# Sixteen loads of 16 to 1 rows that need not end at a row's end, in a log-sum-exp over rows

## Chip, cores, metric

One core of one Trainium2 chip. The metric is device time in microseconds (us), the median of several runs; runs of one kernel here spread over 0.2 to 0.6 us. Times inside a run are counted from the start of its profiled span. A run's reported time is 1.8 us longer than its span.

## The reference

```python
x: (32, 512, 1024) float32, standard normal
max_x = np.max(x, axis=-1, keepdims=True)
out = max_x.squeeze(-1) + np.log(np.sum(np.exp(x - max_x), axis=-1))   # (32, 512) float32
```

That is 16,384 rows of 1,024 elements, 67.1 MB in, 64 KB out. With 128 partitions each holds 128 rows.

## The kernel before

It takes exp without the maximum, sums, takes the logarithm, and guards itself: if a sum is out of range, a slow branch computes everything again. Data come through a ring of 48 row slots per partition. One string is one load. `R6` is six rows exponentiated by one ScalarE instruction and summed by one VectorE reduce; `T2` two rows, exponentiated together, each summed by a VectorE two-input sum of its halves; `A` one row exponentiated and summed by ScalarE alone.

```python
RING = 48
loads = [
    "R6 R5 R5", "R6 R5 R5", "R8 R8", "R8 R4 R4", "R4 R4 R3 R3 A A", "R6 T3 A A A", "R6 A A",
    "R2 A A T2", "R3 R3", "R3", "A A A", "T2 A", "T2", "T2", "T1", "A", "A",
]
...
for i, ops in enumerate(loads):
    size = sum(s for _, s in ops)
    if p + size > RING:
        p = 0
    dma = nc.sync.dma_start(out=ring[:, p : p + size, :], in_=source(c, size)).ins
    for how, s in ops:
        v = ring[:, p : p + s, :]
        sums = sumexp[:, c : c + s]
        if how == "A":
            o = v if c < LAST else last_exp
            exp = nc.scalar.activation(out=o, in_=v, func=AF.Exp, accum_out=sums)
        else:
            exp = nc.scalar.activation(out=v, in_=v, func=AF.Exp)
        ...                          # the reduce or the two-input sums on VectorE
        c += s; p += s
    if c == LATE:                    # 118 rows: first logarithm, first guard check
        ...
```

After the loop:

```python
nc.scalar.activation(out=res[:, W:NC], in_=sumexp[:, W:NC], func=AF.Ln)
nc.sync.dma_start(out=out_rows, in_=res[:, 0:W])
last_store = nc.sync.dma_start(out=out_rest, in_=res[:, W:NC]).ins   # 8 KB: the last store
check(LATE, LAST, 1)                                                 # VectorE, after the last sum
... # small reduce and comparison on VectorE, matmuls, a flag `fine`
all_fine = nc.values_load(fine[0:1, 0:1], engines=ENGINES, ...)      # ScalarE and VectorE read it
with tc.If(all_fine < 1, preferred_fallthrough_block=False):
    ...                                                              # the slow branch
```

## Time and profile before

| | before |
|---|---|
| time, median of 3 | 163.81 us (163.78 to 163.9) |
| span of the profiled run | 161.76 us |
| DMA, first packet to last packet | 1.005 to 157.450 us |
| last load seen landed | 157.954 us |
| last exponential starts | 157.976 us |

The views that show what bounds it are in the prediction. One view of before is shown now: what SyncE waited for at the end (its next step comes at 161.00 in before, 0.76 us ahead of the end of the span; the receiver, what it waited for, us in total, times, longest), and the DMA issue of the last store (KB, us from issue to landing).

```profile
SPq L275 <- DVEq L208: 0.5, 1, 0.5
SPq L275 <- DMA out_dram<-res: 0.4, 1, 0.4
out_dram<-res SPq DMA_DIRECT2D x1, 8.0 KB, 1.6
```

The last thing that SyncE waits for is the 8 KB store, after it has waited for VectorE's branch: in before it has seen everything else by 160.55, and the store at 161.00.

### The profile page before, as it was taken

The numbers are of one execution on the slowest core, as the hardware profiler recorded it, in microseconds if no ns is written. First come the engines' busy times: TensorE is split into PE (matmuls) and PEld (weight loads), VectorE is DVE, ScalarE is ACT, GpSimd is POOL, SyncE is SP. The second block draws the span as 40 slices with busy tenths as digits, with TensorE's granted clock in tenths as the row PEclk, the third lists the DMA queues.
The fourth block names the chain that finished last, engine by engine and source line by source line (L and its number), as shares of the span: only waits on it lengthen the run. The fifth ranks groups of instructions, "written<-read, shape, count | busy, mean of one in ns | idle before, by whom it ended". The sixth has DMA issues, their size and how long they took to land.

```text
span 161.8 us, 221 instructions
## 1 busy us (share of the span) xinstructions
PE 0.8 (0%) x8; PEld 0.3 (0%) x8; DVE 118.5 (73%) x56; ACT 117.2 (72%) x60; POOL 0.2 (0%) x4
## 2 busy tenths in 40 slices
PE   0000000000000000000000000000000000000001
PEld 0000000000000000000000000000000000000000
DVE  0000002999959997299995999999999589799772
ACT  3000069980899609994299924999999999999994
POOL 0000000000000000000000000000000000000000
DMA  7996996997997997998898899889999999999990
GB/s 259 519 519 276 502 519 292 486 519 324 454 519 324 454 519 340 438 519 389 389 519 389 389 519 389 389 389 502 405 389 434 474 389 432 416 428 415 418 368 6
DMA packets 2738, 67.19 MB, mean 415 GB/s; under 512 B 560, under 2 KB 560, under 8 KB 944
## 3 DMA queue, kind: packets, MB, share of 16 engines
q1 hardware_dynamic: 2736, 67.18, 97.0%
q14 instruction: 2, 0.02, 0.0%
HBM read 67.11 MB, written 0.07 MB: 415 GB/s over the span
## 4 chain that ended last, share of the span: by engine, by line
DMA 53%; DVE 35%; ACT 10%; issue 1%; PE 0%
DMA ring<-in_x_dram 53%; DVE sumexp L132 35%; ACT ring L122 9%; ACT ring L120 1%; ACT last_exp L120 0%; PE count L202 0%; DVE fine L203 0%
## 5 line engine op out<-in xcount | busy, mean ns | idle before, releaser
L132 DVE TENSOR_REDUCE sumexp<-ring 128x3 f32<-128x3072 f32 (+5 forms) x21 | 109.5, 5276 | 37.2 <-ACT ring L122 37.2
L122 ACT ACTIVATE ring<-ring 128x3072 f32<-128x3072 f32 (+6 forms) x27 | 100.3, 3763 | 41.4 <-DMA ring<-in_x_dram 41.3
L120 ACT ACTIVATE ring<-ring 128x1024 f32<-128x1024 f32 x14 | 14.6, 1040 | 0.0
L137 DVE SCALAR_TENSOR_TENSOR ring<-ring 128x512 f32<-128x512 f32 x12 | 7.7, 687 | 2.1 <-ACT ring L122 2.1
L120 ACT ACTIVATION_READ_ACCUMULATOR ring<-ring 128x1 f32 x14 | 2.6, 187 | 0.0
L75 ACT ACT_TABLE_LOAD x1 | 1.3, 1283 | 0.8 <-PEq L264 0.8
L102 PE MATMUL count<-far,bad 128*1 128x1 f32 x4 | 0.4, 164 | 158.3 <-DVE clamped L98 158.3
L120 ACT ACTIVATE last_exp<-ring 128x1024 f32<-128x1024 f32 x1 | 1.0, 1027 | 0.0
L137 DVE DVE_READ_ACCUMULATOR ring<-ring 128x1 f32 x12 | 1.0, 83 | 0.0
L76 DVE MEMSET ones<- 128x1 f32 x1 | 0.1, 59 | 0.9 <-PEq L264 0.9
L203 DVE TENSOR_SCALAR fine<-count 1x1 int32<-1x1 f32 x1 | 0.1, 145 | 0.6 <-PE count L202 0.6
L94 DVE TENSOR_SCALAR clamped<-sumexp 128x118 f32<-128x118 f32 (+1 forms) x2 | 0.4, 197 | 0.2
L102 PEld LDWEIGHTS count<-far,bad 128*1 128x1 f32 x4 | 0.2, 81 | 158.4 <-DVE clamped L98 158.4
L98 DVE SCALAR_TENSOR_TENSOR clamped<-clamped,sumexp 128x118 f32<-128x118 f32 (+1 forms) x2 | 0.5, 225 | 0.1
L155 ACT ACTIVATE res<-sumexp 128x112 f32<-128x112 f32 x1 | 0.3, 280 | 0.0
L190 ACT ACTIVATE res<-sumexp 128x16 f32<-128x16 f32 x1 | 0.2, 216 | 0.0
L197 DVE TENSOR_REDUCE bad<-ring 128x1 f32<-128x64 f32 x1 | 0.2, 220 | 0.0
L201 PE MATMUL count<-far,bad 128*1 128x1 f32 x2 | 0.2, 164 | 0.2 <-DVE bad L198 0.2
L202 PE MATMUL count<-ones,sumexp 128*1 128x1 f32 x2 | 0.2, 164 | 0.1
L120 ACT ACTIVATION_READ_ACCUMULATOR last_exp<-ring 128x1 f32 x1 | 0.2, 187 | 0.0
L198 DVE TENSOR_SCALAR bad<-bad 128x1 f32<-128x1 f32 x1 | 0.2, 154 | 0.0
L98 DVE DVE_READ_ACCUMULATOR clamped<-clamped,sumexp 128x1 f32 x2 | 0.2, 82 | 0.0
(7 smaller groups left out, 0.6 us busy)
## 6 DMA issues: line engine op xcount, KB each, us to landing
ring<-in_x_dram SPq DMA_DIRECT2D x1, 6144.0 KB, 28.8
ring<-in_x_dram SPq DMA_DIRECT2D x2, 3072.0 KB, 27.9
ring<-in_x_dram SPq DMA_DIRECT2D x3, 1536.0 KB, 29.2
ring<-in_x_dram SPq DMA_DIRECT2D x1, 4096.0 KB, 27.8
ring<-in_x_dram SPq DMA_DIRECT2D x2, 1024.0 KB, 30.0
ring<-in_x_dram SPq DMA_DIRECT2D x3, 512.0 KB, 25.9
ring<-in_x_dram SPq DMA_DIRECT2D x5, 35.3
out_dram<-res SPq DMA_DIRECT2D x1, 56.0 KB, 8.7
```

The costliest lines, as they stand in the source:

```text
L75: nc.scalar.preload_act_table_set("natural_log_exp_and_others")
L94: nc.vector.tensor_scalar(out=clamped[:, c0:c1], in0=sumexp[:, c0:c1], scalar1=LOW, scalar2=HIGH, op0=ALU.max, op1=ALU.min,)
L98: counted = nc.vector.scalar_tensor_tensor(out=clamped[:, c0:c1], in0=clamped[:, c0:c1], scalar=0.0, in1=sumexp[:, c0:c1], op0=ALU.bypass, ...
L102: nc.tensor.matmul(count, lhsT=bad[:, i : i + 1], rhs=far, start=i == 0, stop=False)
L120: exp = nc.scalar.activation(out=o, in_=v, func=AF.Exp, accum_out=sums)
L122: exp = nc.scalar.activation(out=v, in_=v, func=AF.Exp)
L132: added = [nc.vector.reduce_sum(out=sums, in_=v, axis=AX.X)]
L137: nc.vector.scalar_tensor_tensor(out=lo, in0=lo, scalar=1.0, in1=ring[:, p + r, H:d], op0=ALU.mult, op1=ALU.add, accum_out=sums[:, r : r + 1],
L155: ln = nc.scalar.activation(out=res[:, 0:W], in_=sumexp[:, 0:W], func=AF.Ln)
L190: nc.scalar.activation(out=res[:, W:NC], in_=sumexp[:, W:NC], func=AF.Ln)
L197: nc.vector.reduce_max(out=bad[:, 3:4], in_=last_row[:, 0, 0 : d // 16], axis=AX.X)
L198: nc.vector.tensor_scalar(out=bad[:, 2:3], in0=bad[:, 3:4], scalar1=LOG_LOW, scalar2=None, op0=ALU.is_lt)
```

## The change

Loads are counted in elements, so one may end inside a row. The exponentials take all that has landed, into the unfinished row; the row is summed after the load that completes it. The intent is that ScalarE has as little as possible left when the last loads land, with one load fewer.

```diff
     loads = [
-        "R6 R5 R5", "R6 R5 R5", "R8 R8", "R8 R4 R4", "R4 R4 R3 R3 A A", "R6 T3 A A A", "R6 A A",
-        "R2 A A T2", "R3 R3", "R3", "A A A", "T2 A", "T2", "T2", "T1", "A", "A",
+        (16, "R8 R7 A"), (16, "R8 R7 T1"), (16, "R6 R5 R5"), (16, "R6 R5 R5"), (13.5, "R5 R4 R4"),
+        (12.5, "R7 R6"), (9, "A A A A A A A A A"), (7.5, "R3 R2 R2"), (5.5, "R4 T2"),
+        (4, "A A A A"), (3.5, "T3"), (2.75, "T3"), (2.25, "T2"), (1.5, "T2"), (1, "A"), (1, "A"),
     ]
-    LATE = 118
+    LATE = 119
 ...
-        dma = nc.sync.dma_start(out=ring[:, p : p + size, :], in_=source(c, size)).ins
+        dma = nc.sync.dma_start(out=ring[:, here : here + size], in_=source(done, size)).ins
 ...
             else:
+                upto = end if k + 1 == len(ops) else p + s * d
+                v = ring[:, here:upto]
                 exp = nc.scalar.activation(out=v, in_=v, func=AF.Exp)
+                here = upto
 ...   (the rest turns row indices into element indices)
```

More of the change, by code (lines that the diff above doesn't have):

```diff
@@ L39 @@
     W = NC - B
-    x_rows = x_flat[0 : P * W].rearrange("(p c) d -> p c d", p=P)
-    x_rest = x_flat[P * W : n].rearrange("(p c) d -> p c d", p=P)
+    x_rows = x_flat[0 : P * W].rearrange("(p c) d -> p (c d)", p=P)
+    x_rest = x_flat[P * W : n].rearrange("(p c) d -> p (c d)", p=P)
     out_flat = out.rearrange("a b -> (a b)")
@@ L50 @@
     loads = [
-        "R6 R5 R5", "R6 R5 R5", "R8 R8", "R8 R4 R4", "R4 R4 R3 R3 A A", "R6 T3 A A A", "R6 A A",
-        "R2 A A T2", "R3 R3", "R3", "A A A", "T2 A", "T2", "T2", "T1", "A", "A",
-    ]
-    loads = [[(op[0], int(op[1:] or 1)) for op in load.split()] for load in loads]
-    assert sum(s for ops in loads for _, s in ops) == NC
[3 rows of a table added]
+    ]
+    loads = [
+        (int(size * d), [(op[0], int(op[1:] or 1)) for op in ops.split()]) for size, ops in loads
+    ]
+    assert sum(size for size, _ in loads) == NC * d
+    assert sum(s for _, ops in loads for _, s in ops) == NC
     ENGINES = [mybir.EngineType.Activation, mybir.EngineType.DVE]
-    LATE = 118
+    LATE = 119
     LAST = NC - 1
@@ L62 @@
     psum = ctx.enter_context(tc.tile_pool(name="psum", bufs=1, space=bass.MemoryType.PSUM))
-    ring = big.tile([P, RING, d], fp32, name="ring")
+    ring = big.tile([P, RING * d], fp32, name="ring")
     sumexp = stats.tile([P, NC], fp32, name="sumexp")
@@ L71 @@
     ones = stats.tile([P, 1], fp32, name="ones")
-    last_exp = psum.tile([P, 1, d], fp32, name="last_exp")
+    last_exp = psum.tile([P, d], fp32, name="last_exp")
     count = psum.tile([1, 1], fp32, name="count")
@@ L77, with source @@
     nc.vector.memset(far, 100 * HIGH)
-    def source(c0, size):
-        assert c0 >= W or c0 + size <= W
-        return x_rest[:, c0 - W : c0 - W + size, :] if c0 >= W else x_rows[:, c0 : c0 + size, :]
+    def source(e0, size):
+        assert e0 >= W * d or e0 + size <= W * d
+        return x_rest[:, e0 - W * d : e0 - W * d + size] if e0 >= W * d else x_rows[:, e0 : e0 + size]
     def without_wait(ins, group, reason):
@@ L107 @@
     p = 0
-    for i, ops in enumerate(loads):
-        size = sum(s for _, s in ops)
-        if p + size > RING:
-            p = 0
-        dma = nc.sync.dma_start(out=ring[:, p : p + size, :], in_=source(c, size)).ins
+    here = 0
+    done = 0
+    for i, (size, ops) in enumerate(loads):
+        if here + size > RING * d:
+            assert here == p
+            p = here = 0
+        dma = nc.sync.dma_start(out=ring[:, here : here + size], in_=source(done, size)).ins
         if i == 0:
             first_load = dma
-        for how, s in ops:
-            v = ring[:, p : p + s, :]
+        end = here + size
+        done += size
+        for k, (how, s) in enumerate(ops):
+            rows = ring[:, p : p + s * d].rearrange("p (c d) -> p c d", d=d)
             sums = sumexp[:, c : c + s]
             if how == "A":
+                assert here == p
+                v = ring[:, p : p + d]
                 o = v if c < LAST else last_exp
                 exp = nc.scalar.activation(out=o, in_=v, func=AF.Exp, accum_out=sums)
+                here += d
             else:
+                upto = end if k + 1 == len(ops) else p + s * d
+                v = ring[:, here:upto]
                 exp = nc.scalar.activation(out=v, in_=v, func=AF.Exp)
+                here = upto
+            assert p + s * d <= here <= end
             without_wait(exp, "loads", "the slot's earlier users came before this load")
@@ L131 @@
             if how == "R":
-                added = [nc.vector.reduce_sum(out=sums, in_=v, axis=AX.X)]
+                added = [nc.vector.reduce_sum(out=sums, in_=rows, axis=AX.X)]
             elif how == "T":
                 for r in range(s):
-                    lo = ring[:, p + r, 0:H]
+                    lo = rows[:, r, 0:H]
                     added.append(
                         nc.vector.scalar_tensor_tensor(
-                            out=lo, in0=lo, scalar=1.0, in1=ring[:, p + r, H:d],
+                            out=lo, in0=lo, scalar=1.0, in1=rows[:, r, H:d],
                             op0=ALU.mult, op1=ALU.add, accum_out=sums[:, r : r + 1],
@@ L150 @@
             c += s
-            p += s
+            p += s * d
             last_row = v
+        assert here == end
         tc.add_to_no_dep_group("loads", dma)
@@ L196 @@
     check(LATE, LAST, 1)
-    nc.vector.reduce_max(out=bad[:, 3:4], in_=last_row[:, 0, 0 : d // 16], axis=AX.X)
+    nc.vector.reduce_max(out=bad[:, 3:4], in_=last_row[:, 0 : d // 16], axis=AX.X)
     nc.vector.tensor_scalar(
@@ L214 @@
                     s = min(RING, NC - c0)
-                    v = ring[:, 0:s, :]
+                    v = ring[:, 0 : s * d].rearrange("p (c d) -> p c d", d=d)
                     neg = clamped[:, c0 : c0 + s]
@@ L223 @@
                         nc.scalar.dma_start(
-                            out=ring[:, c1 - c0 : c2 - c0, :], in_=source(c1, c2 - c1)
+                            out=ring[:, (c1 - c0) * d : (c2 - c0) * d],
+                            in_=source(c1 * d, (c2 - c1) * d),
                         ).then_inc(landed, 16)
```

## The prediction

The sum in it came to -0.09 us, from 163.81 to 163.72. Statements that no trace of this case shows are cut out of it, with the cuts marked; no term of the sum is among them, since each was worked out from the trace of before. The figures of that trace, for reading it:

- 1,040 and 7,025 ns are the mean durations of an exponential of one row and of eight. The 0.10 + 0.853 us per row is my estimate; plain exponentials of 2, 3, 4, 5, 6 and 8 rows that follow each other start 1.80, 2.65, 3.51, 4.36, 5.23 and 6.94 us after one another there. Those of one row with its sum start 1.039 us apart (111.549 and 112.588), not 1.036. Reduces of 3, 4, 5, 6 and 8 rows start 3.26, 4.33, 5.39, 6.47 and 8.60 us apart, about 1% more than the 1.055 per row + 0.05 of the walk.
- The first load is issued at 0.00 and its first packet starts at 1.005: the 1 us of issue. The third and the fourth load raise their sixteenth increments at 60.480 and 79.842, 19.36 us apart, as loads of 16 rows do that move one after the other.
- SyncE waited up to 22.7 us for ring slots, and the DMA share was still 1.00 from the first packet to the last.

> **What bounds the kernel now**
>
> I read the page first, then the chain of waits, then the busy time by windows, then the timeline of the last microseconds. The page alone misleads: its chain gives VectorE 35% of the span.
>
> ```profile
> DMA 53%; DVE 35%; ACT 10%; issue 1%; PE 0%
> q1 hardware_dynamic: 2736, 67.18, 97.0%
> ```
>
> The second line is the one that matters: 67.18 MB on one queue keep all 16 DMA engines busy for 97% of the span. To see whether there is a hole anywhere, I cut the span where the first packet starts moving (1.00 us) and where the last packet ends (157.45 us), both read from the trace's records of single packets. Columns: stretch, its length, busy time of PE, PEld, DVE, ACT, POOL, then granted clock, DMA share, GB/s.
>
> ```profile
> 1.00:157.45 156.45, 0.19 (x2) 0.09 (x2) 117.04 (x47) 115.06 (x56) 0.00 (x0) 1.00 1.00 429
> 157.45:161.76 4.31, 0.57 (x6) 0.26 (x6) 1.34 (x8) 1.89 (x5) 0.00 (x0) 1.00 0.04 8
> ```
>
> DMA share 1.00: the loads never pause. So the time is 1.0 us before the first packet, 156.45 us of packets without a hole, and a tail of 4.3 us. DVE's 35% in the chain is only the inferred path by which ring slots came free; it cost nothing, as this piece of the chain in order of time shows (start, length, what):
>
> ```profile
> 27.17 17.35 DVE sumexp L132 x3
> 44.52 0.02 issue
> 44.53 35.31 DMA ring<-in_x_dram
> ```
>
> The fourth load is issued at 44.53 when reduces free its slots, but takes 35.31 us to land, because it queues behind the third load, which is still moving until 60.1. It was ready some 15 us too early; no stall.
>
> What remains is whether the tail begins when the last load lands, or whether ScalarE is then late:
>
> ```profile
> 152.20 4.78 ACT L122 ACTIVATE ring<-ring 128x2048 f32<-128x2048 f32 x3
> 156.88 1.04 ACT L120 ACTIVATE ring<-ring 128x1024 f32<-128x1024 f32 x1
> 157.83 0.19 ACT L120 ACTIVATION_READ_ACCUMULATOR ring<-ring 128x1 f32 x1
> 157.98 1.03 ACT L120 ACTIVATE last_exp<-ring 128x1024 f32<-128x1024 f32 x1
> ```
>
> ScalarE seems busy right up to the last exponential at 157.98. But back-to-back exponentials of one row start 1.036 us apart in this trace, so from 156.88 it could have started at 157.91 or 157.92. The sixteenth semaphore increment of the last load is recorded at 157.954. Hence the landing sets 157.98, by 0.06 us over ScalarE. Taking ScalarE's backlog away alone therefore gains nothing, and the tail after 157.98 (1.15 us of exponential and accumulator, a 0.22 us logarithm, the small store issued at 159.40 and seen landed at 160.99, final barriers) is not touched by the change.
>
> [...]
>
> [...] a packet of 65,536 bytes takes 2.418 us on one engine, 27.1 GB/s, times 16 is 434 GB/s.
>
> [...] Medians here: 4,096 bytes 0.161 us, 8,192 0.312, 12,288 0.461, 24,576 0.913, 49,152 1.815, 65,536 2.418. That is a line, 0.0095 us + 0.1506 us per row of 4 KB, so about 10 ns a packet[...].
>
> [...] Here last packet end to last increment is 157.45 to 157.954, 0.50 us. [...]
>
> [...] 1,040 ns for 1,024 elements[...], 7,025 for 8,192[...]. Issue to issue, I use 0.10 + 0.853 us per row for a plain exponential, and 1.036 for one with its sum.
>
> **The change part by part**
>
> *Seventeen loads become sixteen; bytes are equal (128 rows a partition).* Every load is 128 packets, 8 on each engine, whatever its length; the longest stays 16 rows. From one load's end to the next, the trace has 19.32 us for 16 rows, 9.71 for 8, 7.30 for 6, and about 1.28 for 1 (mean of three): 1.20 us per row plus about 0.09 us per load (8 packets at 10 to 12 ns). One load fewer: -0.09 us. Fractions are multiples of a quarter row, 1,024 bytes, and each stays one run per partition, so 13.5 rows should cost 8 x (0.0095 + 13.5 x 0.1506) = 16.34 us, on the same line.
>
> *Ring reuse.* With 48 slots, the new sizes fill 16+16+16, then 16+13.5+12.5 (six slots unused), then 38 rows. I walked the two engines by row costs (reduce 1.055 us per row + 0.05) and asked when the overlapping reduces free each slot. Load four: free at 45, needed at 60. Load five: 64 against 79. Six: 77 against 96. Seven (9 rows): 97 against 111. Eight: 107.5 against 122. Nine: 112 against 131. Ten: 116 against 137.5; eleven: 124 against 142. The smallest lead is about 14 us. Issue needs 1 us. So the stream should stay without a hole: 0.
>
> *Splitting the exponentials off row ends.* Total ScalarE elements are equal. What changes is that after a short load everything landed is exponentiated at once. I take landings of before at an equal number of loads and shift by 1.20 us a row. Example: before, 123 rows in 13 loads landed at 151.605; now 124.5 rows in 13 loads, so 151.605 + 1.80 = 153.41. Then:
>
> - load 12 (2.75 rows) lands 150.62; ScalarE, free at about 150.6 after the logarithm, works to 150.64 + 0.10 + 2.35 = 153.09;
> - load 13 (2.25) lands 153.41, after ScalarE is idle: starts 153.43, to 155.45;
> - load 14 (1.5) landed 155.30: 155.45 to 156.83;
> - load 15 (1) landed 156.59: 156.83 to 157.87;
> - load 16 (1) lands 156.666 + 1.20 = 157.87: starts at about 157.89.
>
> ScalarE and the last landing meet again within hundredths. The start moves from 157.98 to 157.89: -0.09 us, all from the missing load.
>
> *VectorE's end and the guard.* Load 14's two rows of 0.61 us each come out at 156.94 + 1.31 = 158.25, against 157.99 before. Its check, the small reduction and comparison follow, to about 159.08 instead of 158.82. The last matmul cannot start before ScalarE's sum at about 159.09, so the guard's flag moves by no more than about 0.05 us. SyncE in before had seen everything but the small store by 160.55, and the store at 160.99, so the guard has 0.4 us of slack: 0.
>
> *Instructions.* Reshaped sums (13 one-row two-input sums instead of 12, 19 reduces instead of 21, one-row exponentials with sums 16 instead of 15) shift work between engines with tens of per cent of idle time early on: 0.
>
> Sum: -0.09 us, chosen prediction 163.81 - 0.09 = 163.72 us.
>
> **The rivals**
>
> *Odd packet lengths slow the queue.* Eight of the 16 loads have a fractional length and five end inside a row. For: no such length occurs in before, so nothing measured covers it; 5 ns more in each of the 64 packets an engine gets for them would be +0.3 us (164.0). Against: quarter rows are 1,024 bytes, and lengths from 4 to 64 KB lie on one line.
>
> *A ring wait replaces a row-end wait.* A freshly loaded slot now waits for two exponentials and the reduce over both. For: SyncE's longest wait in before is 22.7 us for reduces, and it issues in order. Against: 14 us of lead everywhere by my walk. If I am wrong by that much, each microsecond of hole adds one: 165 or more.
>
> *ScalarE's backlog was the real bound* and finer loads win 0.3 to 0.5 us: 163.4. For: it has no idle from 138.1 on in before. Against: the 157.954 landing, after which the last exponential starts in 0.02 us.
>
> *ScalarE or VectorE becomes late.* I have ScalarE ready within 0.02 us of the landing; 0.1 us of error in the walk puts the result at 163.8. VectorE would need to be 0.4 us later than I have it.
>
> **Range and chances**
>
> Runs of before spread over 0.12 us, so a step of 0.09 is hardly more than noise. The queue's arithmetic gives a floor of about -0.1 us unless the first load or the skew between engines changes; the rivals reach 0.3 either way. I take 163.45 to 163.92. Two per cent is 3.3 us; only a hole of several microseconds could do that. Faster by over 2%: 0.01; within 2%: 0.98; slower by over 2%: 0.01.
>
> **What would show it right or wrong**
>
> DMA share 1.00 from the first packet to the last, ending at about 157.36; packets of 55,296 bytes at about 2.04 us; ScalarE idle for some 0.3 us before the 2.25-row exponential; the last exponential at 157.9; issue of every load over 10 us before its first packet. Wrong would be a gap between packets, fractional packets above the line, the last exponential well after its landing, or the guard's flag, not the small store, ending the program.

## The result, and the profile after

| | before | after |
|---|---|---|
| time, median of 6 runs each, same rounds | 163.80 us (163.6 to 163.9) | 163.94 us (163.85 to 164.17) |
| ratio | 1 | 1.0012 (1.0000 to 1.0025) |

A ratio is the mean time of one kernel's runs over the mean of the other's runs of the same rounds, so not quite the ratio of the medians. Within 2%, the forecast class; but 163.94 lies just above the range's end of 163.92, and the sign is against the forecast -0.09. The miss of the range is small: a repeat of the same kernel (after_again, below) had a median of 163.82, inside it. The effect is hardly larger than noise, so below I compare single events in the traces rather than times alone.

First the lines of after that answer to those in the prediction: the queues, then the busy time cut at its own first and last packet.

```profile
q1 hardware_dynamic: 2592, 67.18, 96.6%
q14 instruction: 2, 0.02, 0.0%
...
1.02:157.48 156.46, 0.19 (x2) 0.09 (x2) 115.24 (x45) 115.06 (x56) 0.00 (x0) 1.00 1.00 429
157.48:162.14 4.66, 0.43 (x6) 0.22 (x6) 1.68 (x10) 1.82 (x5) 0.00 (x0) 1.00 0.04 7
```

The stream has again no hole (DMA share 1.00, 429 GB/s). It is the tail after it that grew, from 4.31 to 4.66 us. ScalarE at the end of after (start, length, engine, line, instruction, idle time before it):

```profile
153.51 3.50 ACT L137 ACTIVATE ring<-ring 128x2304 f32<-128x2304 f32 x2 [0.24 <-DMA ring<-in_x_dram]
156.92 1.04 ACT L132 ACTIVATE ring<-ring 128x1024 f32<-128x1024 f32 x1
157.86 0.19 ACT L132 ACTIVATION_READ_ACCUMULATOR ring<-ring 128x1 f32 x1
157.96 1.00 ACT L132 ACTIVATE last_exp<-ring 128x1024 f32<-128x1024 f32 x1
```

ScalarE caught up at 153.51, as the change intends, and began the last exponential at 157.96, 0.02 earlier than before. Nothing is lost up to here. VectorE's last row sum is at 157.29 to 157.99 before:

```profile
157.29 0.69 DVE L137 SCALAR_TENSOR_TENSOR ring<-ring 128x512 f32<-128x512 f32 x1
...
157.90 0.08 DVE L137 DVE_READ_ACCUMULATOR ring<-ring 128x1 f32 x1
```

and at 157.66 to 158.36 after:

```profile
157.66 0.68 DVE L154 SCALAR_TENSOR_TENSOR ring<-ring 128x512 f32<-128x512 f32 x1
...
158.27 0.08 DVE L154 DVE_READ_ACCUMULATOR ring<-ring 128x1 f32 x1
```

So VectorE ends 0.37 later. And SyncE's waits and the last store of after:

```profile
SPq L294 <- DMA out_dram<-res: 0.7, 1, 0.7
SPq L294 <- DVEq L226: 0.6, 1, 0.6
out_dram<-res SPq DMA_DIRECT2D x1, 8.0 KB, 2.0
```

The store takes 2.0 us to land instead of 1.6, though it is issued no later (159.36 and 159.40) and nothing in the change touches it. In the traces every load and every store raises its semaphore, the counter that SyncE waits on, 16 times, and has 16 packets of 4 bytes (304 of each for the 19 transfers of before, 288 for the 18 of after). I read this as one increment for each of the 16 DMA engines. The trace's own records of increments and packets, in us from the span's start:

```
                                       before             after
VectorE ends its last row sum          157.987            158.355
8 KB instruction packet, first         159.067-159.635    159.397-159.892
8 KB instruction packet, second        159.595-159.994    159.976-160.443
packets of the last store (64 bytes)   160.239-160.440    160.195-160.500
  15th increment of the store          160.849            160.768
  16th increment of the store          160.985            161.371
end of the span                        161.756            162.143
```

Fifteen increments are there 0.08 us earlier than before; one comes 0.60 us after them. Read by engines, one finishes late. In after the eight data packets of that engine stand alone, one every 7 ns from 160.440, and the second instruction packet ends at 160.443. (The records kept do not number the DMA engines; that the two share one is read from these times.) The packets themselves are little delayed: those of the other fifteen engines, with a 4-byte packet each at the end, are over at 160.409, those of this one at 160.505. But its increment is recorded only 0.87 us after that. That instruction packet is in the page as `q14 instruction`: two packets, 16 KB in all, 0.0% of the DMA time, in both kernels.

**Theory A.** These are fetches of the instruction streams of ScalarE and VectorE. They start when the engines pass a certain place in their streams, near VectorE's last sum, after which both engines go on. VectorE ending 0.37 us later moves its fetch 0.38 us later (159.595 to 159.976), onto the DMA engine and into the moment of the last store, which then completes late.

**Theory B.** The late increment is a chance of one profile, and the lost 0.14 us lie in the loads: fractional packets, another state of the queue.

### The profile page after: what moved, and what is told of

Its sections match the earlier page's. It is cut to its first block, busy times and chain, and to the rows that moved or that the text cites. A ratio compares the mean times of both kernels' runs of the same rounds, so it can differ in the third digit from the quotient of the medians.

```text
span 162.1 us, 222 instructions
## 1 busy us (share of the span) xinstructions
PE 0.6 (0%) x8; PEld 0.3 (0%) x8; DVE 117.0 (72%) x56; ACT 117.1 (72%) x60; POOL 0.2 (0%) x4
## 4 chain that ended last, share of the span: by engine, by line
DMA 63%; ACT 18%; DVE 13%; another core or an unknown queue 3%; SPq 0%; issue 0%; PE 0%; DVEq 0%
DMA ring<-in_x_dram 63%; ACT ring L137 18%; DVE sumexp L149 12%; DVE ring L154 1%; SPq L120 0%; PE count L219 0%; DVE clamped L100 0%; DVE bad L216 0%; DVE bad L215 0%; DVE clamped L104 0%; DVE fine L221 0%; PE count L220 0%; DVEq L100 0%
## 5 line engine op out<-in xcount | busy, mean ns | idle before, releaser
L149 DVE TENSOR_REDUCE sumexp<-ring 128x5 f32<-128x5120 f32 (+6 forms) x19 | 107.3, 5704 | 37.7 <-ACT ring L137 37.7
L137 ACT ACTIVATE ring<-ring 128x5120 f32<-128x5120 f32 (+14 forms) x25 | 99.0, 4014 | 41.4 <-DMA ring<-in_x_dram 41.4
L132 ACT ACTIVATE ring<-ring 128x1024 f32<-128x1024 f32 x15 | 15.6, 1040 | 0.0
L154 DVE SCALAR_TENSOR_TENSOR ring<-ring 128x512 f32<-128x512 f32 x13 | 8.4, 688 | 3.5 <-ACT ring L137 3.5
L104 DVE SCALAR_TENSOR_TENSOR clamped<-clamped,sumexp 128x119 f32<-128x119 f32 (+1 forms) x2 | 0.5, 226 | 0.1
```

Source lines behind the costliest of these rows:

```text
L104: counted = nc.vector.scalar_tensor_tensor(out=clamped[:, c0:c1], in0=clamped[:, c0:c1], scalar=0.0, in1=sumexp[:, c0:c1], op0=ALU.bypass, ...
L149: added = [nc.vector.reduce_sum(out=sums, in_=rows, axis=AX.X)]
L154: nc.vector.scalar_tensor_tensor(out=lo, in0=lo, scalar=1.0, in1=rows[:, r, H:d], op0=ALU.mult, op1=ALU.add, accum_out=sums[:, r : r + 1],)
```

## The experiments

All are correct by the comparison with the reference and were timed over five rounds beside before.

| run | time, median | before, median | ratio (95% interval) |
|---|---|---|---|
| after_again | 163.82 | 163.69 | 1.0009 (0.9995 to 1.0022) |
| dve_pad | 164.06 | 163.69 | 1.0021 (1.0007 to 1.0034) |
| act_pad | 164.19 | 163.69 | 1.0029 (1.0016 to 1.0043) |
| before_r1 | 163.97 | 163.69 | 1.0016 (1.0003 to 1.0030) |
| before_wide | 164.35 | 163.67 | 1.0041 (1.0029 to 1.0053) |
| after_short | 163.56 | 163.67 | 0.9991 (0.9978 to 1.0003) |
| after_lean | 163.64 | 163.67 | 0.9995 (0.9982 to 1.0008) |
| whole16 | 164.04 | 163.67 | 1.0016 (1.0003 to 1.0029) |
| pad_d3a3 | 164.47 | 163.62 | 1.0044 (1.0030 to 1.0057) |
| pad_d5a3 | 163.78 | 163.62 | 1.0012 (0.9998 to 1.0026) |
| pad_d5 | 163.62 | 163.68 | 0.9998 (0.9986 to 1.0011) |
| pad_d6 | 163.57 | 163.68 | 0.9996 (0.9983 to 1.0009) |

And the events of the tail in each profiled run, worked out from the records of packets and increments as above (us; "VectorE's last sum" is its end; "late" is the 16th increment minus the 15th; the last column but one is the 16th increment minus the end of VectorE's fetch):

```
              VectorE's  VectorE's        store:                 16th -    span
              last sum   fetch            15th     16th    late  fetch end
before        157.99     159.60-159.99    160.85   160.99  0.14  0.99      161.76
after         158.36     159.98-160.44    160.77   161.37  0.60  0.93      162.14
after_again   158.22     159.84-160.29    160.64   161.22  0.58  0.93      161.99
act_pad       158.71     160.32-160.69    161.18   161.67  0.49  0.98      162.44
before_wide   158.72     160.41-160.74    161.04   161.78  0.75  1.05      162.56
after_short   157.85     159.62-160.13    160.80   161.00  0.20  0.87      161.77
whole16       158.64     160.01-160.56    161.07   161.57  0.51  1.02      162.35
pad_d3a3      158.76     160.57-160.88    161.23   161.92  0.68  1.04      162.69
pad_d5a3      158.65     159.92-160.36    161.12   161.26  0.14  0.90      162.05
pad_d5        158.45     159.71-160.16    160.88   161.20  0.32  1.04      161.97
pad_d6        158.22     159.45-159.98    160.64   161.01  0.37  1.03      161.78
dve_pad       158.31     156.29-156.63    161.65   161.68  0.04  -         162.45
after_lean    158.33     after the store  160.71   160.74  0.03  -         161.84
before_r1     158.48     after the store  160.76   160.77  0.01  -         161.99
```

**after_again**: no edit.

> The changed kernel unchanged, a control for a difference of 0.2 us. Theory A (the new tail: VectorE ends 0.37 us later, so an 8 KB instruction fetch that follows it is still on one DMA engine when the 8 KB result store comes, and that engine's semaphore increment is late): the last increment of the last store comes again some 0.6 us after the fifteenth, near 161.3 to 161.4 us, and the time is 0.1 to 0.3 us above the kernel before. Theory B (a chance of that one profile; the time difference comes from the load stream): the sixteenth increment follows the others within 0.2 us this time, while the time stays 0.1 to 0.3 above.

The sixteenth increment came 0.58 us after the fifteenth again, at 161.22. Theory B's chance is out. This profile's last exponential started at 157.82, 0.14 earlier than in the first profile of after: that much a single profile varies.

**dve_pad and act_pad**: eight tiny instructions at the start, where the engine idles.

```diff
     nc.vector.memset(far, 100 * HIGH)
+    pad = stats.tile([P, 8], fp32, name="pad")
+    for k in range(8):
+        nc.vector.memset(pad[:, k : k + 1], 0.0)                                    # dve_pad
+        nc.scalar.activation(out=pad[:, k : k + 1], in_=ones, func=AF.Exp)          # act_pad instead
```

> Changed kernel plus eight tiny VectorE memsets at the start, where VectorE idles for 26 us. If the late fetch belongs to VectorE's instruction stream and comes at a fixed count of instructions, it comes eight instructions earlier (some 1.5 to 5 us earlier), misses the store, and the time falls by 0.3 to 0.4 us to about 163.55. If it is tied to the end of the stream, to a branch or to another engine, nothing moves: within 0.1 us of after_again, and the fetch stays at about 159.4.

> Changed kernel plus eight tiny ScalarE exponentials at the start, where ScalarE idles for 20 us. If the late fetch belongs to ScalarE's instruction stream by count, it comes several us earlier and the time falls by 0.3 to 0.4 us; if it belongs to VectorE or to a branch, nothing moves: within 0.1 us of after_again.

Each moved exactly one of the two fetches forward: memsets moved the second (about 159.9) to 156.29, exponentials the first (about 159.3) to 151.66. The other fetch stayed in the tail, 0.3 to 0.6 us later than in after and after_again (at 159.87 and 160.32), as the tail itself was. So the first is ScalarE's, the second VectorE's, and each moves with added instructions before it. With VectorE's fetch gone from the tail, the store landed as one:

```profile
158.85 1.03 ACT L135 ACTIVATE last_exp<-ring 128x1024 f32<-128x1024 f32 x1 [0.85 <-DMA ring<-in_x_dram]
...
out_dram<-res SPq DMA_DIRECT2D x1, 8.0 KB, 1.4
```

1.4 us to landing, the sixteenth increment only 0.04 late. But both runs were slower, against the hoped-for gain, and the first of these two lines says why: ScalarE sat 0.85 us waiting for the last load. Fifteen of its increments were there by 157.84, the sixteenth at 158.83, 0.99 late, and the exponential started 0.02 us after that one, at 158.85. The fetch that falls inside the loads here goes with one late increment. In act_pad the sixteenth increment of the last load was 0.38 late, and VectorE's fetch still met the store. The fetch's own packet took 0.33 us in dve_pad; why the delay reached 0.99 is open.

**before_r1**: one row's sum by a reduce.

```diff
-"T2", "T2", "T1", "A", "A",
+"T2", "T2", "R1", "A", "A",
```

> The kernel before with one edit: the single row of its fifteenth load is summed by a one-row reduce in place of the two-input sum, so VectorE ends some 0.4 us later (158.4 instead of 157.99), all loads and exponentials as before. Theory A: the fetch moves from 159.07 to about 159.4 to 159.5, the store's last increment from 160.99 to about 161.4, and the time rises by 0.3 to 0.4 us to about 164.15. Theory B (VectorE's end has 0.4 us of slack and the loss lies in the load stream of the changed kernel): within 0.1 us of the kernel before.

Slower by 0.16%, as much as theory A asked in sign, but by another way, so this run does not prove it. A two-input sum is two instructions in the trace (in before 12 sums and 12 reads of their accumulators), a reduce one (21, without a read). With one instruction fewer VectorE's fetch came only at 161.56, after the store, and the store landed in 1.4 us. ScalarE's fetch was still there: its packet ended at 160.03, 0.16 us before the store's packets began, yet no increment came late, and the last one came 0.74 us after that packet's end. So what VectorE's fetch does to the store, ScalarE's did not do here. What held the end up instead:

```profile
SPq L275 <- DVEq L208: 1.2, 1, 1.2
...
out_dram<-res SPq DMA_DIRECT2D x1, 8.0 KB, 1.4
```

SyncE waited 1.2 us for VectorE's branch, against 0.5 before. The flag was 0.23 later, and VectorE's branch came 1.04 us after it began to read the flag, instead of 0.62.

**before_wide**: the same delay of VectorE without a change in the number of instructions.

```diff
-"T2", "T2", "T1", "A", "A",
+"T2", "T2", "W1", "A", "A",
+            elif how == "W":
+                row = ring[:, p, :]
+                added = [nc.vector.scalar_tensor_tensor(
+                    out=row, in0=row, scalar=0.0, in1=row,
+                    op0=ALU.mult, op1=ALU.add, accum_out=sums)]
```

> The kernel before, the single row of its fifteenth load summed by one two-input sum over 1,024 elements (element times zero plus element, result correct) in place of 512: same number of instructions, VectorE ends some 0.5 us later. Theory A: both late fetches move by 0.4 to 0.5 us, the second to about 160.1 to 160.5 where the result store moves; the store's sixteenth increment comes 0.4 us or more after the fifteenth; time +0.3 to +0.5 us over before. Theory B (VectorE has 0.4 us of slack, the loss is in the loads): +0.1 us at most.

```profile
157.49 1.22 DVE L136 SCALAR_TENSOR_TENSOR ring<-ring 128x1024 f32<-128x1024 f32 x1
...
SPq L283 <- DMA out_dram<-res: 0.8, 1, 0.8
...
out_dram<-res SPq DMA_DIRECT2D x1, 8.0 KB, 2.2
```

One sum of 1.22 instead of 0.69 us, on an engine that is busy 73% of the time, and the kernel before lost 0.68 us by the medians. Its fetch moved by 0.81 to 160.41, and the sixteenth increment came 0.75 late. The loss is more than the 0.5 I expected at most: in this profile the loads also landed 0.19 later (158.141 against 157.954), for which I have no cause. That would account for the part over 0.5: the wide sum itself took 0.53 us longer and began 0.20 later (157.49 against 157.29).

**after_short**: the reverse. The two sums of the fourteenth load are cut to half their width. Two of 128 columns are wrong on purpose, still within the comparison's tolerance.

```diff
-                    lo = rows[:, r, 0:H]
+                    w = H // 2 if i == 13 else H
+                    lo = rows[:, r, 0:w]
 ...
-                            out=lo, in0=lo, scalar=1.0, in1=rows[:, r, H:d],
+                            out=lo, in0=lo, scalar=1.0, in1=rows[:, r, H : H + w],
```

> The changed kernel with the two sums of its fourteenth load cut to half their width (two of 128 columns wrong on purpose, the guard still content): same instructions, loads and exponentials, VectorE ends some 0.5 us earlier, at about 157.65. Theory A: both fetches move back by 0.4 to 0.5 us, end before the store's packets, the sixteenth increment follows the fifteenth within 0.2 us, time -0.3 to -0.45 us against the changed kernel, about 0.1 us below before (163.6 where before is 163.7). Theory B: within 0.1 us of the changed kernel.

```profile
157.42 0.42 DVE L155 SCALAR_TENSOR_TENSOR ring<-ring 128x256 f32<-128x256 f32 x1
...
158.11 0.17 DVE L100 TENSOR_SCALAR clamped<-sumexp 128x8 f32<-128x8 f32 x1 [0.26 <-ACT ring L132]
...
out_dram<-res SPq DMA_DIRECT2D x1, 8.0 KB, 1.6
```

VectorE ended 0.51 us earlier than in after, its fetch was over at 160.13, the increment was 0.20 late, and the store took 1.6 us. The median fell to 163.56, below before though not clear of it; 163.82 to 163.56 is -0.26 us against after_again, in another set of rounds. The expected -0.3 to -0.45 was a little too much. A likely part of the reason is that VectorE's check now waits 0.26 us for ScalarE's sum; the fetch came 1.77 us after VectorE's last sum instead of 1.62.

**after_lean**: fewer instructions early, where both engines have time.

```diff
-(16, "R8 R7 A"), (16, "R8 R7 T1"),
+(16, "R8 R8"), (16, "R8 R8"),
```

> The changed kernel with its first two loads worked as R8 R8 each: three ScalarE and two or three VectorE instructions fewer, at a place where both engines have 14 us of slack; everything from the third load on as it was. Theory A with fetches at a fixed count of instructions: both fetches come later, after the small store's packets (160.6 or later, or not before the end), the store is not disturbed, time -0.3 to -0.4 us against the changed kernel, 163.4 to 163.6, below before. If a later fetch now holds up an engine's last branch instead, or still meets the store, nothing is gained: within 0.1 us of the changed kernel. Theory B: within 0.1 us.

Both fetches went past the store (161.26 and 161.59), and the store landed in 1.4 us, its increments together. The median was 163.64, about 0.2 us below after_again. The rest of the gain was given back at the branches, as one of the expectations allowed: ScalarE's first step after its comparison came 0.40 us after it instead of 0.08, and VectorE's second comparison 0.51 us after the step before it instead of 0.10. The span ended 1.10 us after the store instead of 0.77.

**whole16**: the reach into unfinished rows taken away, sixteen loads kept.

```diff
-(13.5, "R5 R4 R4"), (12.5, "R7 R6"), (9, ...), (7.5, "R3 R2 R2"), (5.5, "R4 T2"),
-(4, ...), (3.5, "T3"), (2.75, "T3"), (2.25, "T2"), (1.5, "T2"), (1, "A"), (1, "A"),
+(14, "R5 R5 R4"), (12, "R6 R6"), (9, ...), (7, "R3 R2 R2"), (6, "R4 T2"),
+(4, ...), (3, "T3"), (3, "T3"), (2, "T2"), (2, "T2"), (1, "A"), (1, "A"),
```

> Sixteen loads with the changed kernel's plan, but every load a whole number of rows (14, 12, 9, 7, 6, 4, 3, 3, 2, 2, 1, 1 after the four of 16): only the reach into unfinished rows is taken away. By the walk, ScalarE starts the last exponential at 158.16 instead of 157.89, since it ends the last two-row load at 157.12; loads land as in the changed kernel; VectorE ends some 0.25 us later too. So 0.2 to 0.35 us above the changed kernel, about 164.1. If fractional loads cost the queue something, the last landing would come earlier here than in the changed kernel by 0.1 us or more.

```profile
155.38 1.91 ACT L137 ACTIVATE ring<-ring 128x2048 f32<-128x2048 f32 x1 [0.39 <-DMA ring<-in_x_dram]
157.20 1.04 ACT L132 ACTIVATE ring<-ring 128x1024 f32<-128x1024 f32 x1
...
158.24 1.01 ACT L132 ACTIVATE last_exp<-ring 128x1024 f32<-128x1024 f32 x1
```

The last load had landed at 157.88, but ScalarE reached it at 158.24: two whole rows are too much work after 155.38. So the reach does what it is meant to; with sixteen loads it saves about 0.3 us at the last exponential. The median, 164.04, is 0.22 above after_again's, in other rounds, as expected. The last landing is no earlier than in after (157.88 against 157.91 and 157.78), so fractional loads cost the queue nothing that shows. The scheduler also put the small reduction ahead of the check here, so VectorE's tail is not the same in order.

**pad_d3a3 and pad_d5a3**: three exponentials on ScalarE, three or five memsets on VectorE, as in dve_pad. They were run on another chip.

> The changed kernel plus three tiny memsets on VectorE and three tiny exponentials on ScalarE at the start. [...] three instructions bring the fetches forward by a few tenths of a microsecond to one or two microseconds, into the stretch after the last load packet (157.4) and before the store's packets (160.1), when the DMA engines are idle. Expected: both fetches between 157.5 and 159.9, the store's sixteenth increment within 0.15 us of the fifteenth, near 160.75; end at about 161.55; time -0.35 to -0.45 us against the changed kernel, about 163.45, 0.1 to 0.25 below before. If a fetch falls before 157.4 it delays a load on one engine instead, and the time is no better than the changed kernel's.

> The same with five memsets on VectorE. Eight put its fetch at 156.3, inside the loads, and delayed the last landing by 1 us. Five should put it at about 157.5 to 159: if after 157.5, as good as with three, about 163.45; if before, the last landing is late on one engine and the time is 163.8 or more.

A miss; how far three or five instructions move a fetch was my estimate from the runs with eight. Three exponentials moved ScalarE's fetch to 151.7 and 151.6, as far as eight had, inside the loads; the last load's sixteenth increment came 0.46 and 0.29 us after its fifteenth. Three memsets, on the other hand, did not bring VectorE's fetch forward at all: in pad_d3a3 it came 1.82 us after its last sum, against 1.62 in after, and with five memsets 1.27. So the place moves with added instructions, but not in proportion to their number; why is not tested. In pad_d3a3 the sixteenth increment of the store came 0.68 late, in pad_d5a3, where VectorE's fetch was over 0.13 us before the store's packets, only 0.14 late.

**pad_d5 and pad_d6**: memsets on VectorE alone.

> The changed kernel plus five tiny VectorE memsets at the start and nothing on ScalarE. In the run with five memsets and three exponentials VectorE's fetch came 1.23 us after its last semaphore wait (1.58 us in the changed kernel) and ended before the store's packets, whose sixteenth increment then came only 0.14 us late; what spoilt that run was ScalarE's fetch inside the loads. Without the ScalarE part: ScalarE's fetch at about 159.3 to 159.9 as in the changed kernel, VectorE's at about 159.5 to 160.05, last landing at 157.9, the store's sixteenth increment within 0.2 us of the fifteenth; time -0.2 to -0.4 us against the changed kernel, about 163.5, at or just below before.

> The same with six memsets: VectorE's fetch at 158.5 to 159.6 if it keeps moving forward by instructions, further from the store: 163.4 to 163.5, 0.1 to 0.2 below before. If it jumps to 157 or earlier, as with eight, one engine's load packets are late and the time is 163.8 or more.

VectorE's fetch came 1.26 and 1.23 us after its last sum instead of 1.62, but no further forward with six than with five. Both medians lie 0.06 and 0.11 below before, inside the noise, and 0.2 below after_again, in other rounds on another chip. The store's sixteenth increment was still 0.32 and 0.37 late, although the fetch packets had ended before the store's packets began. That gave the last piece: in all eleven runs where VectorE's fetch falls between the last load and the store's increments, the sixteenth increment comes 0.87 to 1.05 us after the fetch packet *ends*. Measured from the end of the store's own 64-byte packets the same increments scatter more widely, over 0.55 to 0.99 us. No version tried here beats before clear of the noise.

## Why the prediction was wrong, point by point

**The load stream, -0.09: not contradicted, but too small to read in one run.** In the runs without a fetch inside the loads, first packet to last packet takes 156.45, 156.41 and 156.65 us with seventeen loads (before, before_r1, before_wide; mean 156.50) and 156.31 to 156.52 with sixteen (seven runs; mean 156.42). That is -0.08, but single runs of one kind differ by 0.2, so the agreement is no proof. The forecast end of the stream, 157.36, was 157.48 in the first profile of after and 157.32 in the second, against 157.45 in before. The median packet of 55,296 bytes took 2.041 us, as forecast. The rival "odd lengths slow the queue" found 9,216, 11,264 and 14,336 bytes 3 to 4 ns above the line, where it asked for 5 in all 64 packets, and the four longest fractional lengths within 2 ns of it; the sum does not show it.

**Ring reuse, 0: right.** The loads were issued at 45.3, 64.5, 77.9, 97.3, 108.0, 112.4, 116.7 and 124.8, within 1 us of the walk.

**ScalarE's walk: right within the scatter.** Predicted 153.43 for the 2.25-row exponential and 157.89 for the last; measured 153.51 and 157.96, and 157.82 for the last in the repeated profile.

**VectorE's end: right.** Predicted 158.25, measured 158.36 and 158.22. The flag: predicted at most +0.05, measured +0.11 and -0.03.

**"so the guard has 0.4 us of slack: 0": this step failed.** With it failed the claim that the small store and what follows it "is not touched by the change". The guard's own chain did have slack: in after SyncE had seen everything but the store by 160.66 and the store only at 161.39. But VectorE's end has a second consumer that I did not look for. Its last sum is followed, 1.6 us later, by a fetch of 8 KB of its instructions on one DMA engine, and the last store's sixteenth increment follows the end of that fetch by 0.87 to 1.05 us. In before this was already what ended the program: the sixteenth increment, 160.985, is 0.14 after the fifteenth and 0.99 after the fetch. So VectorE had no slack at all against the end, and its 0.26 (measured 0.37 and 0.23) went through in full: the span grew by 0.39 in the first profile and by 0.23 in the second. The sum should have been: the loads' -0.09 does not reach the end, because the fetch and not the store's issue ends it; VectorE's +0.26 does. That makes 164.07, worked out afterwards; the medians of after are 163.94 and 163.82. The timed difference (+0.14 and +0.13) is smaller than the profiled one (+0.39 and +0.23). Before was profiled once, in a run of 163.55 that is faster than all but five of the 46 timed runs of before, so part of the gap may be that; it stays open. The range was also too narrow for a step of this size: it went by a spread of 0.12 us in three runs of before, and later sets of 6 to 11 runs spread over 0.3 to 0.46.

**What is shown and what is not.** Shown: the two fetches belong to the two engines (the pads move one each, to 156.29 and to 151.66); VectorE's end moves its fetch and with it the store's last increment and the end, in both directions at an unchanged number of instructions (before_wide: fetch end 159.99 to 160.74, increment 160.99 to 161.78; after_short against after: 160.44 to 160.13, 161.37 to 161.00). Not shown: why the increment waits. The 0.87 to 1.05 us from the fetch's end to the increment is a measured interval, not a cause. In before_r1 and after_lean branches are late by 0.3 to 0.4 us, but there the fetch packets begin 0.45 to 0.62 us after the same engine's last branch has ended (161.56 against 161.11 in before_r1). So no run here shows a branch that waits for its fetch, and why these branches were late stays open. Open too is why ScalarE's fetch in before_r1 held no increment back. What exactly triggers a fetch is open, since three and eight added instructions on ScalarE gave the same place, and three on VectorE moved nothing forward.

## What to carry to other kernels

Slack measured along the data path was not slack against the end here: ask of the last engine to finish also what follows in its instruction stream, and whether a DMA that the program doesn't name shares an engine with the last load or store. Where a store is late, look at its sixteen increments one by one; fifteen on time and one late, by 0.60 us here, pointed to another transfer, read from the times as one on the same DMA engine, and not to bandwidth. When variants differ by tenths of a per cent, as here, the number of instructions on an engine, not only their length, can move such a fetch (eight memsets moved VectorE's by 3.7 us here), so compare variants at an equal number, or take the shift into account.
